# In the chunked scans of an RWKV-7 layer, VectorE masks each bank of scores before ScalarE copies from it, where ScalarE copied first

## The chip, the cores and the metric

The kernel runs on one core of a Trainium2 chip. A core has TensorE (PE, the matrix engine), VectorE (DVE), ScalarE (ACT), GpSimd (POOL) and SyncE (SP, which issues most transfers). Each engine takes its own instructions strictly in order and runs beside the others; semaphores make one wait for another. TensorE writes its results into PSUM, which has eight banks; ScalarE and VectorE read them from there. The metric is the time of one execution on the device in microseconds (us), lower being better, as the median of several runs.

## The reference

Two layers run on 2048 latent tokens with a context of 256 tokens, width 1024. Layer 0 is an RWKV-7 mixer, layer 1 a differential attention. The change lies in the scans of layer 0: for each of 16 heads of 64, in both directions of time,

```python
def step(S, inp):
    r_t, w_t, k_t, v_t, kk_t, a_t = inp
    sa = jnp.einsum("bhvk,bhk->bhv", S, kk_t)
    S = (S * w_t[:, :, None, :]
         - sa[..., None] * (kk_t * a_t)[:, :, None, :]
         + v_t[..., None] * k_t[:, :, None, :])
    return S, jnp.einsum("bhvk,bhk->bhv", S, r_t)
...
oc_f, sc_f = scan_direction(con, 0, s0, False)
oc_b, sc_b = scan_direction(con, 1, s0, True)
ol_f, _ = scan_direction(lat, 0, sc_f, False)
ol_b, _ = scan_direction(lat, 1, sc_b, True)
```

## The kernel before

A first stage projects the tokens and writes streams to HBM; `phase2` runs the scans; a readout and the attention layer follow. `phase2` works by chunks of 64 tokens: 36 chunks in each direction make 72 turns of a loop over `q`, and the two directions alternate. A turn does two things that are nine turns apart in the scan:

- **`scores` for chunk `q+9`.** Four banks of score products, g0 to g3 here, each of four matmuls (L680) into a PSUM tile `ps` named `scps`. Everything else is read out of that bank. ScalarE copies the two diagonal blocks to `A32` (L687, two copies) and an off-diagonal block to `E` (L690); these are "the copies". VectorE multiplies the bank by a causal mask, one half into `L` (L691, the tile LA for g0 and g1, LB for g2 and g3), the other half into `Pb` (L692); these are "the masks".
- **`chain` for chunk `q`.** TensorE multiplies the state by LA and LB (L796, "x", the first matmuls of a turn) into the two `xops` tiles; ScalarE copies to `X` (L798); TensorE multiplies by the inverse `U` (L804); ScalarE scales into `RS` (L807, "the RS scaling"); TensorE forms the state update (L813, needs `RS` and the keys `KB`) and the outputs (L818, needs `RS` and `Pb`); VectorE updates the state `RX` (L824, L825) and ScalarE copies the outputs (L826, "the RS copies"). There are two `xops` tiles, so the next turn's x can't begin before the first RS copy has emptied the first of them. The chunk's `v` comes by a transfer into `RS` that SP issues after it has issued the store of the turn before (L827), which waits for the RS copies.

Beside these, `turned` transposes keys into `scps` banks (L773) and ScalarE copies them to `KB` (L774), before g0 and again between g1 and g2. `scps` has three banks, taken in turn, so g2 needs the bank of g0 emptied by both its readers, and g3 that of g1.

Every four turns, the blocks of four chunks are inverted together. By `q mod 4` I call the turns kind 0 to 3:

- kind 0: `join`: VectorE negates `Dg` into `U` (L742, four instructions) between the masks of g0 and g1; TensorE joins (L749); ScalarE copies `U` (L751).
- kind 1: nothing more.
- kind 2: `unpack`: VectorE transposes the inverse (L715 before the masks of g0, L717 between those of g0 and g1, L719 between those of g2 and g3).
- kind 3: VectorE transposes `A32` to `N` for GpSimd's inversion (L699, L700) and unpacks the last piece (L721) ahead of the masks of g0; TensorE joins rows (L733); then a `join` as in kind 0. There is one `A32`, so ScalarE's first copy of this turn waits for L700.

The order of all four engines is the order in which this code is written (`in_order` fixes it), and the framework adds the waits: the second reader of a bank waits for the first, on whichever engine each is. The order of the steps in a turn is

```python
MAIN = "ubgjugbcgujgc"
```

after a first step of the chain, with u for `unpack`, b for `turned`, g for a bank of scores, j for `join`, c for the chain.

Of the kernel before, what the change touches and what calls it, by code (L numbers as in the profile page):

```python
# [15 lines left out]
ALU = mybir.AluOpType  # L16
# [17 lines left out]
def bcast(ap, dim, n):  # L34

    ap = ap.unsqueeze(dim)
    shape = list(ap.shape)
    shape[dim] = n
    return ap.broadcast_to(shape)
# [561 lines left out]
def causal_masks(k, pool):  # L601

    nc = k.nc
    mk = pool.tile([128, 2, 2, 64], F32, name="causal")
    nc.vector.memset(mk, 1.0)
    for d in range(2):
        for slot in range(2):
            strict = slot == d
            for half in range(2):
                v = mk[half * 64:half * 64 + 64, d, slot]  # L610
                step = 1 if d == 0 else -1
                nc.gpsimd.affine_select(out=v, in_=v, pattern=[[step, 64]], base=-1 if strict else 0,
                                        channel_multiplier=-step, compare_op=ALU.is_ge, fill=0.0)
    return mk
# [7 lines left out]
def phase2(k):  # L622

    nc, tc, S = k.nc, k.tc, k.S
# [3 lines left out]
    with ExitStack() as st:  # L628
# [17 lines left out]
        krow = (HI, LO)  # L646
# [22 lines left out]
        def scores(d, par, loaded, A32, E, Pb):  # L669

            LA, LB, BA, BB = loaded
            yield LA, LB, Pb
            br, kr = brow[d], krow[d]
            for ab in range(2):
                L, B = ((LA, BA), (LB, BB))[ab]
                for q in range(2):
                    ps = sc.tile([128, 4, 2, 64], F32, name="scps")
                    for j in range(4):
                        p = 4 * q + j
                        nc.tensor.matmul(f2(ps[:, j]), f2(B[:, p]), f2(L[:, p]), start=(j == 0), stop=True,  # L680
                                         skip_group_check=True)
                    prs = slice(4 * q, 4 * q + 4)
                    h0 = 8 * ab + 4 * q
                    c0 = 16 * par + h0
                    for blk in range(2):
                        r = slice(br.start + 32 * blk, br.start + 32 * blk + 32)
                        nc.scalar.copy(A32[r, :, c0:c0 + 4].rearrange("p t c -> p c t"),  # L687
                                       ps[r, :, d, 32 * blk:32 * blk + 32])
                    e, ec = (slice(0, 32), slice(32, 64)) if d == 0 else (slice(96, 128), slice(0, 32))
                    nc.scalar.copy(E[e, c0:c0 + 4, :], ps[e, :, d, ec])  # L690
                    nc.vector.tensor_tensor(L[krow[ab], prs], ps[kr], bcast(mk[kr, d], 1, 4), op=ALU.mult)  # L691
                    nc.vector.tensor_tensor(Pb[br, h0:h0 + 4], ps[br, :, 1 - d], bcast(mk[br, d, 1 - d], 1, 4),  # L692
                                            op=ALU.mult)
                    yield

        def invert(A32, eng):
# [139 lines left out]
        for i in range(LEAD + 1):  # L836
# [3 lines left out]
            if i == 0:  # L840
                mk = causal_masks(k, ca)
# [30 lines left out]
        with in_order(k, mybir.EngineType.PE, mybir.EngineType.DVE, mybir.EngineType.Activation, mybir.EngineType.Pool):  # L872
            for q in range(-LEAD, nq):
# [21 lines left out]
                if s < nq:  # L895
                    if s % 4 == 0:
                        tiles[s // 4] = [ip.tile([128, 32, 32], F32, name="A32", bufs=1),
                                         ip.tile([128, 32, 32], F32, name="E", bufs=2), None]
                    A32, E, _ = tiles[s // 4]
                    if s % 2 == 0:  # L900
                        Pb = pb.tile([128, 16, 64], F32, name="Pb")
                    g = scores(s % 2, s // 2 % 2, loaded.pop(s), A32, E, Pb)
                    prep[s] = step(g)
# [791 lines left out]
```

## Time and profile before

| | |
|---|---|
| median of 3 runs | 4957.97 us (4957.65 to 4968.01) |
| the profiled execution's own time | 4959.93 us |
| its span | 4958.2 us |
| busy over the span | PE 94%, PEld 84%, DVE 74%, ACT 54%, POOL 22% |
| mean granted TensorE clock | 0.972 |

The span is the profiled part of the execution; 1.7 us of its own time lie around it. PE is the matmuls and PEld the weight loads, which overlap them. A matmul's end is modelled, so a share of PE near 100% doesn't say that PE has nothing to gain. The scans run from 1167 us, where the first bank of scores is read, to 2273 us, where the last output is stored. A row of the time line names the engine, the line of the kernel, the operation and the tiles; what stands in brackets is how long the engine was idle before it and what ended that.

### The profile page before, as it was taken

To read this page: it belongs to the slowest core of one execution; us is meant where nothing else is said; L and a number is where in the kernel's file an instruction comes from. 1 tells how busy PE (TensorE), PEld (TensorE's weight loads), DVE (VectorE), ACT (ScalarE), POOL (GpSimd) and SP (SyncE) were. 2 spreads that over 40 slices of the span, in tenths; PEclk is the share of its full clock that TensorE was granted. 3 is DMA by queue.
4 is the path that set the end of the run, shared out by engine and by line. 5 is a ranking of instruction groups with operands and counts; after the bars stand their busy time and mean duration, and the time that the engine had idled before them with its cause. 6 is when DMAs were issued, how large, how long until landed. Compare 5 with 4: busy or idle time off the path is not lost. (4 is left out here: it accounts for less than half of the span.)

```text
span 4958.2 us, 100487 instructions
## 1 busy us (share of the span) xinstructions
PE 4642.4 (94%) x40786; PEld 4181.3 (84%) x40786; DVE 3676.0 (74%) x5933; ACT 2678.6 (54%) x4780; POOL 1110.3 (22%) x1470
## 2 busy tenths in 40 slices
PE   7999999998889998898989999999999999999989
PEld 5999999996788888876768888878888888888977
DVE  6788887888877777766768258238888888888843
ACT  4555655554666666655541221227777777777720
POOL 1121112112555665551222022010000000000000
PEclk8999999999999999999999999999999999999999
DMA  4555665557666667669853332241212112111042
GB/s 165 169 166 168 179 182 160 165 166 212 155 157 168 159 168 169 166 189 283 265 172 100 113 112 90 94 116 29 52 32 49 49 33 49 49 32 30 19 158 94
DMA packets 733584, 629.94 MB, mean 127 GB/s; under 512 B 175238, under 2 KB 638521, under 8 KB 732097
## 3 DMA queue, kind: packets, MB, share of 16 engines
q1 hardware_dynamic: 730641, 619.84, 44.1%
q8 instruction: 322, 5.28, 0.4%
q10 hardware_dynamic: 2480, 3.67, 0.3%
q14 instruction: 141, 1.16, 0.1%
HBM read 423.61 MB, written 199.77 MB: 126 GB/s over the span
## 5 line engine op out<-in xcount | busy, mean ns | idle before, releaser
L1423 ACT ACTIVATE p<-p,m 128x2304 f32<-128x2304 f32 x256 | 568.9, 2222 | 92.9 <-DVE p L1412 88.6
L1455 PE MATMUL pv<-v,at 128*128 128x128 f32 x4608 | 598.6, 275 | 3.1 <-ACT at L1450 3.0
L1455 PEld LDWEIGHTS pv<-v,at 128*128 128x128 f32 x4608 | 555.1, 192 | 4.2 <-ACT at L1450 4.2
L1409 PE MATMUL sc<-ks,qh 128*128 128x512 f32 (+1 forms) x1280 | 520.1, 406 | 5.1 <-DVE p L1412 4.2
L1450 ACT COPY at<-tps 128x512 f32<-128x512 f32 (+1 forms) x640 | 343.7, 537 | 273.8 <-PE tps L1448 272.5
L1410 PE MATMUL sc<-ks,ql 128*128 128x512 f32 (+1 forms) x1280 | 464.2, 372 | 0.0
L363 PE MATMUL mmps<-hH,wH 128*128 128x386 f32 x1632 | 433.4, 346 | 17.6 <-DVE sg L581 12.7
L363 PE MATMUL mmps<-hL,wH 128*128 128x386 f32 x1632 | 431.0, 344 | 8.4 <-DVE hL L92 8.4
L363 PE MATMUL mmps<-hH,wL 128*128 128x386 f32 x1632 | 428.1, 343 | 0.3 <-DVE nm_ss L197 0.3
L939 PE MATMUL mmps<-wH,hH 128*128 128x512 f32 x1088 | 425.1, 391 | 3.1 <-ACT hH L91 3.1
L939 PE MATMUL mmps<-wH,hL 128*128 128x512 f32 x1088 | 424.4, 390 | 1.4 <-DVE hL L92 1.4
L939 PE MATMUL mmps<-wL,hH 128*128 128x512 f32 x1088 | 424.7, 390 | 0.0
L1412 DVE TENSOR_SCALAR_CACHE_REDUCE p<-sc,m 128x1280 f32<-128x1280 f32 x256 | 396.3, 1548 | 17.5 <-PE sc L1410 1.3
L1433 DVE SCALAR_TENSOR_TENSOR p<-p,r,p 128x1152 f32<-128x1152 f32 x256 | 373.4, 1459 | 4.5
L1412 DVE TENSOR_SCALAR_CACHE_REDUCE p<-sc 128x1024 f32<-128x1024 f32 x256 | 312.6, 1221 | 62.3 <-PE sc L1410 60.4
L1448 PE MATMUL tps<-ident,p 128*128 128x128 f32 x2304 | 355.9, 272 | 0.3
L363 PEld LDWEIGHTS mmps<-hH,wH 128*128 128x128 f32 x1632 | 300.7, 193 | 21.8 <-DVE sg L581 16.1
L1486 POOL TENSOR_TENSOR o<-o,sub_y 128x512 f32<-128x512 f32 (+1 forms) x33 | 33.5, 1014 | 1272.5 <-DVE sub_y L1481 1270.6
L363 PEld LDWEIGHTS mmps<-hL,wH 128*128 128x128 f32 x1632 | 303.6, 192 | 10.4 <-DVE hL L92 9.2
L1448 PEld LDWEIGHTS tps<-ident,p 128*128 128x128 f32 x2304 | 278.0, 141 | 36.4 <-ACT at L1450 1.4
L363 PEld LDWEIGHTS mmps<-hH,wL 128*128 128x128 f32 x1632 | 304.1, 192 | 0.9 <-DVE nm_ss L197 0.8
L707 POOL TENSOR_TENSOR N<-N,rank 128x30 f32<-128x30 f32 (+14 forms) x510 | 280.0, 549 | 40.0
(309 smaller groups left out, 10348.9 us busy)
## 6 DMA issues: line engine op xcount, KB each, us to landing
wr<-in_rw_in_dram SPq DMA_DIRECT2D x102, 512.0 KB
s_qr<-QR SPq DMA_DIRECT2D x48, 768.0 KB
BK<-s_bk SPq DMA_DIRECT2D x72, 512.0 KB
s_bk<-BK SPq DMA_DIRECT2D x47, 768.0 KB
wraw<-in_da_in_dram SPq DMA_DIRECT2D x64, 512.0 KB
BA<-s_bk SPq DMA_DIRECT2D x72, 256.0 KB
LA<-s_qr SPq DMA_DIRECT2D x72, 256.0 KB
BB<-s_bk SPq DMA_DIRECT2D x72, 256.0 KB
```

The lines of the kernel that those rows point to most:

```text
L363: nc.tensor.matmul(a[:, :b1 - b0], wt[:, kt, :], ht[:, kt, b0:b1], start=(kt == 0 and wt is wH and ht is hH), stop=(kt == KT - 1 and last))
L707: eng.tensor_tensor(N[:, m + 1:32, 0:m], N[:, m + 1:32, 0:m], t, op=ALU.subtract)
L939: k.nc.tensor.matmul(ps, s(kt), m(kt), start=(kt == 0 and s is sH and m is mH), stop=(kt == KT - 1 and last))
L1409: nc.tensor.matmul(s[:, b0 - g0:b1 - g0], qh[:, cs], ks, start=True, stop=False)
L1410: nc.tensor.matmul(s[:, b0 - g0:b1 - g0], ql[:, cs], ks, start=False, stop=True)
L1412: nc.vector.tensor_scalar(tiles[n][c][:, g0:g1], s[:, :g1 - g0], -1.0, m, op0=ALU.mult, op1=ALU.min, accum_out=least)
L1423: nc.scalar.activation(P, P, AF.Exp, bias=m, scale=-1.0, accum_out=z)
L1433: nc.vector.scalar_tensor_tensor(P0[:, b0:b1], P1[:, b0:b1], r, P0[:, b0:b1], op0=ALU.mult, op1=ALU.add)
L1448: nc.tensor.transpose(ps[:, c - b0:c - b0 + 128], P0[:, c:c + 128], k.ident)
L1450: (eng.copy if eng is nc.scalar else eng.tensor_copy)(at[b][:, :b1 - b0], ps[:, :b1 - b0])
L1455: nc.tensor.matmul(acc, at[b][:, c - b0:c - b0 + 128], H.v[:, c // 128], start=(c == 0), stop=(c == T - 128))
L1486: eng.tensor_tensor(H.o[:, cs], H.o[:, cs], bcast(y[:, cs.start - t0:cs.stop - t0], 2, 128), op=ALU.mult)
```

## The change

In `scores`, the two masks on VectorE stand ahead of the three copies on ScalarE. Nothing else is altered: the instructions, their sizes and their order on each engine are the same, since the copies are ScalarE's and the masks VectorE's. What differs is who waits for whom. The line numbers move: masks L691, L692 become L685, L686, and copies L687, L690 become L690, L693.

```diff
@@ scores
                     c0 = 16 * par + h0
+                    nc.vector.tensor_tensor(L[krow[ab], prs], ps[kr], bcast(mk[kr, d], 1, 4), op=ALU.mult)
+                    nc.vector.tensor_tensor(Pb[br, h0:h0 + 4], ps[br, :, 1 - d], bcast(mk[br, d, 1 - d], 1, 4),
+                                            op=ALU.mult)
                     for blk in range(2):
                         r = slice(br.start + 32 * blk, br.start + 32 * blk + 32)
                         nc.scalar.copy(A32[r, :, c0:c0 + 4].rearrange("p t c -> p c t"),
                                        ps[r, :, d, 32 * blk:32 * blk + 32])
                     e, ec = (slice(0, 32), slice(32, 64)) if d == 0 else (slice(96, 128), slice(0, 32))
                     nc.scalar.copy(E[e, c0:c0 + 4, :], ps[e, :, d, ec])
-                    nc.vector.tensor_tensor(L[krow[ab], prs], ps[kr], bcast(mk[kr, d], 1, 4), op=ALU.mult)
-                    nc.vector.tensor_tensor(Pb[br, h0:h0 + 4], ps[br, :, 1 - d], bcast(mk[br, d, 1 - d], 1, 4),
-                                            op=ALU.mult)
                     yield
```

VectorE in a turn of kind 2 in the middle of the scans, before, with the engines that each instruction waits for (PE, Activation for ScalarE, Pool; the number behind is the program's). LA and LB take the first mask of a bank, Pb the second.

```order
L715 STREAM_TRANSPOSE Tt<-N 32x32x32 [waits Pool_49]
L691 TENSOR_TENSOR LA_11137<-scps,causal 64x512 [waits PE_49,Activation_49]
L692 TENSOR_TENSOR Pb<-scps,causal 64x256
L717 STREAM_TRANSPOSE Tt<-N 32x32x32
L691 TENSOR_TENSOR LA_11137<-scps,causal 64x512 [waits PE_49,Activation_49]
L692 TENSOR_TENSOR Pb<-scps,causal 64x256
```

The same place now.

```order
L715 STREAM_TRANSPOSE Tt<-N 32x32x32 [waits Pool_49]
L685 TENSOR_TENSOR LA_11137<-scps,causal 64x512 [waits PE_49]
L686 TENSOR_TENSOR Pb<-scps,causal 64x256
L717 STREAM_TRANSPOSE Tt<-N 32x32x32
L685 TENSOR_TENSOR LA_11137<-scps,causal 64x512 [waits PE_49]
L686 TENSOR_TENSOR Pb<-scps,causal 64x256
```

Nothing has moved; the masks' wait for ScalarE is gone, and only that for TensorE is left.

ScalarE in the same turn, before, from the copies of g1 to those of g2; the copies of g3 and the two RS copies follow in both. RS belongs to the chain, KB to the keys.

```order
L687 COPY A_18036<-scps 32x4x32 [waits PE_49]
L687 COPY A_18036<-scps 32x4x32
L690 COPY E<-scps 32x128
L774 COPY KB<-scps 128x512 [waits PE_49]
L807 ACTIVATE RS<-chps 64x512 [waits DMAHW7_49,PE_49,Activation_49]
L807 ACTIVATE RS<-chps 64x512
L687 COPY A_18036<-scps 32x4x32 [waits PE_49]
L687 COPY A_18036<-scps 32x4x32
L690 COPY E<-scps 32x128
```

The same place now.

```order
L690 COPY A_18036<-scps 32x4x32 [waits DVE_49,PE_49]
L690 COPY A_18036<-scps 32x4x32
L693 COPY E<-scps 32x128
L774 COPY KB<-scps 128x512 [waits PE_49]
L807 ACTIVATE RS<-chps 64x512 [waits DMAHW7_49,PE_49,Activation_49]
L807 ACTIVATE RS<-chps 64x512
L690 COPY A_18036<-scps 32x4x32 [waits DVE_49,PE_49]
L690 COPY A_18036<-scps 32x4x32
L693 COPY E<-scps 32x128
```

The order is the same here too; the first copy out of every bank now also waits for VectorE, and what stands behind it in ScalarE's queue (the key copy, the RS scaling, the RS copies) stands behind that wait.

## Rows read from the trace of the kernel before

**Rows 1.** Waits, 1300 to 2160 us: total us, times, longest.

```profile
DVE LA L691 <- ACT E L690: 106.3, 43, 7.0
...
PE chps L813 <- DMA RS<-s_v: 23.7, 22, 2.6
```

**Rows 2.** Groups by line, 1300 to 2160 us: busy us, mean ns of one.

```profile
L687 ACT COPY A<-scps 32x128 f32<-32x128 f32 x478 | 178.6, 374 | 60.4 <-PE scps L680 40.0 <-DVE N L700 11.8 <-PE chps L804 2.4
...
L692 DVE TENSOR_TENSOR Pb<-scps,causal 64x256 f32<-64x256 f32 x237 | 100.0, 422 | 3.2
...
L691 DVE TENSOR_TENSOR LA<-scps,causal 64x512 f32<-64x512 f32 x119 | 81.7, 686 | 107.7 <-ACT E L690 106.3
...
L774 ACT COPY KB<-scps 128x512 f32<-128x512 f32 x120 | 69.8, 582 | 1.9 <-PE scps L773 0.5
...
L826 ACT COPY RS<-xops 64x512 f32<-64x512 f32 x118 | 68.4, 579 | 129.7 <-PE xops L818 129.7
L690 ACT COPY E<-scps 32x128 f32<-32x128 f32 x238 | 65.9, 277 | 1.4
```

**Rows 3.** Time line of PE: start of x in turns 4, 32 to 36, 60.

```profile
1313.85 1.15 PE L796 MATMUL xops<-RX,LA 128*64 128x64 f32 x32
...
1720.89 1.15 PE L796 MATMUL xops<-RX,LA 128*64 128x64 f32 x32
...
1733.88 1.15 PE L796 MATMUL xops<-RX,LA 128*64 128x64 f32 x32
...
1747.16 1.15 PE L796 MATMUL xops<-RX,LA 128*64 128x64 f32 x32
...
1758.69 1.15 PE L796 MATMUL xops<-RX,LA 128*64 128x64 f32 x32
...
1775.75 1.15 PE L796 MATMUL xops<-RX,LA 128*64 128x64 f32 x32
...
2125.29 0.92 PE L796 MATMUL xops<-RX,LA 128*64 128x64 f32 x24
```

**Rows 4.** Time line of ScalarE and VectorE, turn 32 (kind 0).

```profile
1724.49 0.78 ACT L687 COPY A<-scps 32x128 f32<-32x128 f32 x2 [0.31 <-PE scps L680]
...
1726.56 2.72 DVE L742 TENSOR_SCALAR U<-Dg 32x512 f32<-32x512 f32 x4
...
1726.96 1.21 ACT L807 ACTIVATE RS<-chps 64x512 f32<-64x512 f32 x2
...
1729.81 1.16 ACT L751 COPY U<-chps 32x512 f32<-32x512 f32 x2 [0.75 <-PE chps L749]
...
1733.05 0.58 ACT L826 COPY RS<-xops 64x512 f32<-64x512 f32 x1 [1.18 <-PE xops L818]
```

**Rows 5.** Time line of PE, turn 33 (kind 1).

```profile
1744.08 1.15 PE L813 MATMUL chps<-RS,KB 128*64 128x64 f32 x32 [1.76 <-DMA RS<-s_v]
```

**Rows 6.** Time line of ScalarE and VectorE, turn 34 (kind 2).

```profile
1750.77 0.76 ACT L687 COPY A<-scps 32x128 f32<-32x128 f32 x2 [0.25 <-PE scps L680]
...
1757.13 1.96 DVE L719 STREAM_TRANSPOSE Dg<-N 64x1024 f32<-64x1024 f32 x1
```

**Rows 7.** Time line, turn 35 (kind 3).

```profile
1760.70 2.21 PE L733 MATMUL chps<-Tt,E 32*32 32x32 f32 x128
...
1766.17 1.96 DVE L721 STREAM_TRANSPOSE Dg<-N 64x1024 f32<-64x1024 f32 x1
...
1766.42 0.77 ACT L687 COPY A<-scps 32x128 f32<-32x128 f32 x2 [1.52 <-DVE N L700]
...
1769.03 1.87 DVE L742 TENSOR_SCALAR U<-Dg 32x512 f32<-32x512 f32 x4
```

**Rows 8.** Start of x in turns 27 and 28.

```profile
1641.41 1.15 PE L796 MATMUL xops<-RX,LA 128*64 128x64 f32 x32
...
1661.93 1.15 PE L796 MATMUL xops<-RX,LA 128*64 128x64 f32 x32
```

**Rows 9.** Windows, four us of turn 27: busy us by engine, PEclk, DMA share, GB/s.

```profile
1656.00:1660.00 4.00, 4.00 (x53) 3.64 (x50) 1.26 (x3) 2.13 (x5) 3.45 (x8) 0.55 0.00 0
```

## The prediction

> **What bounds the kernel now.** I began with the waits of the scans' steady part, 1300 to 2160 us [rows 1]. In 43 of 119 masks into LA VectorE sat idle until ScalarE's last copy out of the same bank, 106.3 us in all: this is the wait that the change takes away. It is no gain by itself, since nothing says that anybody waits for VectorE there. So the second view is the time line of a round of four turns, and what ends each turn: the next x, whose starts are in [rows 3]. Turns 32 to 35 lasted 12.99, 13.28, 11.53 and 17.06 us (kinds 0 to 3), 54.86 us together, a round in which the matmuls are seen at full speed. From turn 4 to turn 60, 14 rounds, it is 811.44 us, or 57.96 a round: on the average 3.10 us are lost beside it.
>
> What the reader is to see in [rows 4]: ScalarE has some room in a turn. It waited 0.75 us before the copies of `U` and 1.18 us before the first RS copy, in each case for TensorE. It is TensorE that carries the turns (in kind 1 it waits 1.76 us for the transfer of `v` [rows 5]), and ScalarE feeds it at three places of the chain. VectorE's work is in lumps: 2.72 us of `U` between the masks of g0 and g1 in kind 0 [rows 4], transposes of 1.96 us at the same place and ahead of g3's masks in kind 2 [rows 6]. Before, ScalarE ran past these lumps. Now each copy stands behind them.
>
> **The change part by part.** No instruction is added or removed; only the order within a bank turns round, so its cost is the difference of two queues. The pieces, from [rows 2]: the copies of a bank are 2 x 0.374 + 0.277 = 1.03 us, its masks 0.686 + 0.422 = 1.11, and 1.15 with the step to the next instruction; a key copy is 0.58, an RS copy 0.58. The RS scaling is 1.21 and the `U` copies 1.16 [rows 4]. I lay out each kind of turn in the times of the trace: VectorE masks as soon as the bank is there or it is free, the copies follow, everything else keeps its place.
>
> Kind 0 [rows 4]: g0 is there at 1724.49, when ScalarE took it up. Masks to 1725.64, the four L742 (2.72) to 1728.36, masks of g1 to 1729.51. ScalarE, which before had begun g1's copies by 1725.5, ends them at 1730.54, the key copy at 1731.13, the RS scaling at 1732.35 (it had ended at 1728.17), g2's copies at 1733.4, `U` at 1734.55, g3's at 1735.6, the first RS copy at 1736.2. From then on x can start, at about 1736.3 instead of 1733.88: **+2.4 us**. Is TensorE ready by then? In kind 1 the update began 3.08 us before the next x [rows 5, 3], and its second half needs the end of the scaling, so from 1732.35 it is ready 3.08 less half an update (0.54), at 1734.9. ScalarE's queue decides, by 1.4 us. The banks don't: g3 waits for g1's copies (1730.54), and ScalarE comes to g3 four us later.
>
> Kind 1: VectorE has no lump. Each bank's copies come some 1.15 us later, but the update waited 1.76 us for `v` [rows 5], and the transfer is issued behind the RS copies of the turn before, which have moved with x. The delay lies beside that wait: **0**. Without this cover it would be up to 1.15 us a turn.
>
> Kind 2 [rows 6]: g0 is there at 1750.77. Masks to 1751.92, L717 (as long as L719, 1.96) to 1753.9, g1's masks to 1755.05 and g2's to 1756.2, L719 to 1758.15, g3's to 1759.3. ScalarE: g1's copies to 1756.1, keys 1756.7, scaling 1757.9, g2's copies 1758.95, g3's, which wait for the masks, to 1760.35, RS copy 1760.95, x at 1761.05 instead of 1758.69: **+2.35**. TensorE would be ready at 1757.9 + 2.54 = 1760.45.
>
> Kind 3 [rows 7]: here something comes back. VectorE began L719 at 1757.13 and now begins at 1756.2, 0.93 earlier, and its queue from there is the same, so L721 ends at 1766.17 + 1.96 - 0.93 = 1767.2. With x at 1761.05, g0 is there 3.60 us later as in kind 0 (1724.49 - 1720.89), plus 2.21 for joining rows, at 1766.85; VectorE is last. Masks to 1768.35, the four L742 (1.87 here) to 1770.2, g1's masks to 1771.35, copies to 1772.4, keys 1773.0, scaling 1774.2, g2's copies 1775.25, `U` 1776.4, g3's 1777.45, RS copy 1778.05, x 1778.15. Before it was 1775.75, and with the 2.35 that the turn starts later 1778.10: **+0.05**. ScalarE's new wait costs what it saves by no longer waiting 1.52 us for L700.
>
> A clean round becomes 4.8 us longer. Banks are scored up to turn 62, 63 turns or 15.75 rounds, so there are 16 turns each of kinds 0 and 2 and 15 of kind 3: 16 x 2.4 + 16 x 2.35 + 15 x 0.05 = 76.8 us. In the nine turns ahead of the chain nothing on ScalarE is waited for by a chain, and I count nothing.
>
> Against this stands a part of the 3.10 us a round that are lost now, mostly in stretches at half the clock [rows 9]. TensorE gets slack of 1.4, 0.6 and 1.4 us in kinds 0, 2 and 3 (ready 1734.9, 1760.45 and 1776.75 against x), and slow matmuls ahead of such slack cost nothing. Bounds: nothing is hidden (0), or as much as the slack, all of the 3.10 (48.8 over 15.75 rounds). I take 1 us a round, a third, since a slow stretch falls anywhere in a round and the slack lies at three turns' ends: -16. **Sum: 76.8 - 16 = +61 us**, on 4959.93 of the profiled execution 5021, and as that stands 2 us above the median, **5019 us** at the median.
>
> **The rivals.** *The clock falls more often* (slower still). Each of the new waits leaves TensorE idle for one to two us. The granted clock was 0.55 over four us of turn 27 [rows 9], near the lower of its two levels of 1.2 and 2.4 GHz, and that turn lasted 20.52 us [rows 8] where one of the same kind lasted 17.06: 3.46 us for such a stretch. One more of them a round is 54.5 us: 5073. For it speaks that waits become more; against it, that waits of about this length are all over the scans now and most turns are not slowed. [...]
>
> *VectorE is the one that ends last* (faster). If the copies' delay found room, what would be left is VectorE running ahead: in kind 3 ScalarE waited 1.52 us for L700 [rows 7], and 15 times that is 22.8 us: 4935. It decides on the lump between the masks of g0 and g1: ScalarE's room in kind 0 is 0.75 + 1.18 = 1.93 us, and its g1 copies begin 4.0 us late (1729.51 against 1725.5). With a lump of 0.6 us instead of 2.72 it would be free. I see no way to that.
>
> *The waits are hidden everywhere as in kind 1* (no change, 4958): if TensorE waited for `v` in all turns. That wait is 23.7 us [rows 1] over some 60 turns (119 masks into LA, two a turn), 0.4 us a turn, against 2.4 needed.
>
> *Only one of the two kinds shows* (half: 4985 to 4995), for instance if L742 takes 1.87 us in kind 0 as it does in kind 3, and x finds the bank free sooner.
>
> **How the numbers follow.** The forecast has 0.62 (4995 to 5045 by the bounds of what is hidden and some tenths of a us in each step), the clock 0.16, half 0.07, no change 0.08, faster 0.07. A measurement here can tell some 0.2%, 10 us, from no change. So faster 0.07, same 0.09 with a little of the half, slower 0.84. The range 4985 to 5060 holds the forecast, the half and the lower part of the clock's case, about 0.8.
>
> **What would show it.** After: no wait of LA for `E`; instead ScalarE's first copy of a bank waits for `Pb`, longest before g1 in kinds 0, 2 and 3. Turns of kinds 0 and 2 last some 15.4 and 13.9 us, kinds 1 and 3 as before. PE waits for the first RS copy before x. Everything after the scans is only shifted. I'd be wrong if ScalarE still reached the RS copies before TensorE's outputs, or if kind 3 grew or shrank by more than a us.

## The result and the profile after

With the masks first the kernel takes 5030.74 us (median of 4 runs, 5024.96 to 5040.06) against 4957.81 for the kernel before (4 runs on the same chip): a ratio of 1.0142, interval 1.0121 to 1.0163, or 73 us more. The ratios here and below are estimates from all the runs and differ from the quotients of the medians by up to 0.0011. The profiled execution took 5031.1 us, with a span of 5029.4 and a mean granted clock of 0.962, where it was 0.972. Of all the executions behind the numbers below one, of the second kernel under "Which banks cost?", took 12099.97 us at a granted clock of 0.60; it is left out.

The waits of the kernel after, over the same stretch and with the same columns as [rows 1]:

```profile
ACT A L690 <- DVE Pb L686: 186.4, 108, 3.4
DVE LA L685 <- PE scps L680: 133.4, 47, 6.5
...
PEld scps L680 <- ACT E L693: 65.7, 60, 2.0
...
PE scps L680 <- ACT E L693: 50.7, 41, 1.8
ACT RS L826 <- PE xops L818: 48.8, 71, 2.1
...
PE chps L813 <- DMA RS<-s_v: 9.2, 10, 1.8
...
PE xops L796 <- ACT RS L826: 4.8, 11, 0.5
```

The wait of LA for `E` is gone, and VectorE now waits 133.4 us for the bank itself: it runs ahead of TensorE. In its place ScalarE waits 186.4 us for `Pb`. The reader should look at what stands under these: TensorE's scores (L680) now wait for `E`, up to 1.8 us at a time, a wait that the same stretch of the kernel before does not have. That is the bank of g2 or g3 being emptied too late by copies that now come last. Over turns 4 to 59 it is 20.5 us in the 14 turns of kind 0, 23.9 in those of kind 2 and 7.9 in those of kind 3, or some 1.5, 1.7 and 0.6 us a turn. ScalarE's wait for TensorE's outputs before the RS copies has gone from 129.7 us in 118 places [rows 2] to 48.8 in 71, and before x TensorE waits for the first RS copy only 4.8 us in all. The wait for `v`, the cover of kind 1, has shrunk from 23.7 to 9.2 us.

The time line of ScalarE in turn 8 (kind 0; its x starts at 1375.91), which answers to [rows 4]:

```profile
1380.72 0.76 ACT L690 COPY A<-scps 32x128 f32<-32x128 f32 x2 [1.52 <-DVE Pb L686]
...
1384.62 0.75 ACT L690 COPY A<-scps 32x128 f32<-32x128 f32 x2 [3.03 <-DVE Pb L686]
1385.19 0.29 ACT L693 COPY E<-scps 32x128 f32<-32x128 f32 x1
1385.50 0.59 ACT L774 COPY KB<-scps 128x512 f32<-128x512 f32 x1
1385.99 1.21 ACT L807 ACTIVATE RS<-chps 64x512 f32<-64x512 f32 x2
...
1390.42 0.58 ACT L826 COPY RS<-xops 64x512 f32<-64x512 f32 x1 [0.30 <-PE xops L818]
```

And VectorE beside it:

```profile
1379.51 0.68 DVE L685 TENSOR_TENSOR LA<-scps,causal 64x512 f32<-64x512 f32 x1 [2.84 <-PE scps L680]
...
1380.66 2.73 DVE L742 TENSOR_SCALAR U<-Dg 32x512 f32<-32x512 f32 x4
1383.41 0.68 DVE L685 TENSOR_TENSOR LA<-scps,causal 64x512 f32<-64x512 f32 x1
```

The lump of L742 stands between the two masks into LA, and ScalarE waits 3.03 us before g1's copies for it and for g1's masks behind it. Behind them the key copy and the RS scaling start late: 1385.99 is 10.08 us behind x, where in [rows 3, 4] it was 6.07 (1726.96 against 1720.89).

TensorE in turns 5 to 9:

```profile
1333.58 1.15 PE L796 MATMUL xops<-RX,LA 128*64 128x64 f32 x32
...
1345.42 1.15 PE L796 MATMUL xops<-RX,LA 128*64 128x64 f32 x32
...
1354.27 1.16 PE L680 MATMUL scps<-LB,BB 128*128 128x128 f32 x8 [1.79 <-ACT E L693]
...
1359.15 1.15 PE L796 MATMUL xops<-RX,LA 128*64 128x64 f32 x32
...
1375.91 1.15 PE L796 MATMUL xops<-RX,LA 128*64 128x64 f32 x32 [0.47 <-ACT RS L826]
...
1381.81 1.16 PE L680 MATMUL scps<-LB,BB 128*128 128x128 f32 x8
...
1385.53 1.91 PE L680 MATMUL scps<-LB,BB 128*128 128x128 f32 x8 [1.43 <-ACT E L693]
1387.37 1.95 PE L813 MATMUL chps<-RS,KB 128*64 128x64 f32 x32
1389.25 2.08 PE L818 MATMUL xops<-RS,Pb 64*64 64x64 f32 x32
1391.25 1.15 PE L796 MATMUL xops<-RX,LA 128*64 128x64 f32 x32
...
1400.14 1.15 PE L813 MATMUL chps<-RS,KB 128*64 128x64 f32 x32 [0.62 <-DMA RS<-s_v]
```

Two things are to be seen. Turns 5 to 7 (kinds 1 to 3) last 11.84, 13.73 and 16.76 us, so this kind 1 is shorter than the 13.28 of [rows 3]; but it is the shortest of fourteen, and their mean is 13.68. And in turn 8 TensorE waits 1.43 us for `E` before g3, and the matmuls behind that wait take 1.91 and 1.95 us, where the same forms take 1.16 and 1.15 elsewhere. From there L813, L818 and the next x follow one another without a wait. The windows (columns as in [rows 9]) of those four us and of 30 us that end ten us ahead of them:

```profile
1385.00:1389.00 4.00, 3.47 (x38) 3.25 (x40) 1.79 (x4) 3.89 (x10) 3.53 (x7) 0.59 0.17 34
...
1345.00:1375.00 30.00, 26.28 (x597) 24.44 (x595) 27.07 (x34) 19.17 (x45) 9.77 (x20) 1.00 0.65 160
```

The granted clock is 0.59 in the one, near the lower level of 1.2 GHz, and 1.00 in the other, in which TensorE had also waited 1.79 us (at 1354.27). Over turns 4 to 60, from x to x, the window of the kernel before is:

```profile
1313.85:2125.29 811.44, 726.33 (x14787) 680.42 (x14785) 629.56 (x869) 526.51 (x1232) 472.94 (x870) 0.96 0.67 165
```

and that of the kernel after:

```profile
1318.10:2193.50 875.40, 781.22 (x14786) 725.14 (x14786) 633.80 (x870) 523.51 (x1232) 466.74 (x868) 0.91 0.62 153
```

The mean round went from 57.96 to 62.53 us (875.40 / 14), and 4.57 us over 15.75 rounds are 72 us. By the traces 64 of the 71 us between the two spans lie in these turns, and 4 more ahead of turn 4. By kind, the mean of the 14 turns from x to x:

| us | kind 0 | kind 1 | kind 2 | kind 3 |
|---|---|---|---|---|
| before | 13.67 | 13.29 | 12.52 | 18.49 |
| after | 16.56 | 13.68 | 14.35 | 17.94 |

The busy time of the other engines is the same to 1.3%, but TensorE was busy 54.9 us longer with the same matmuls, at a clock of 0.91 instead of 0.96. From the two levels, a mean of 0.96 is 8% of the time at half the clock, some 65 us here, and 0.91 is 18%, some 158 us.

### The profile page after: what moved, and what is told of

It is laid out like the page before. It is cut to its first block, busy times and chain, and to the rows that moved or that the text cites. A ratio compares the mean times of both kernels' runs of the same rounds, so it can differ in the third digit from the quotient of the medians.

```text
span 5029.4 us, 100489 instructions
## 1 busy us (share of the span) xinstructions
PE 4707.4 (94%) x40786; PEld 4234.1 (84%) x40786; DVE 3681.6 (73%) x5933; ACT 2676.9 (53%) x4780; POOL 1103.2 (22%) x1470
## 3 DMA queue, kind: packets, MB, share of 16 engines
q14 instruction: 140, 1.15, 0.1%
## 5 line engine op out<-in xcount | busy, mean ns | idle before, releaser
L690 ACT COPY A<-scps 32x128 f32<-32x128 f32 x576 | 214.6, 373 | 274.8 <-DVE Pb L686 253.0
```

## The experiments

My theory was that ScalarE's queue behind VectorE's lumps makes the turns longer, and that the clock costs little. The main rival was that the new waits of TensorE bring the clock down. All ratios are to the kernel before on the same chip.

**Which banks cost?** Masks first only in g1 of kinds 0, 2 and 3, copies first in the other 13 banks of a round; then just the opposite set.

```diff
+                    first = (kind, ab, q) in ((0, 0, 1), (2, 0, 1), (3, 0, 1))
+                    if first:
+                        nc.vector.tensor_tensor(L[krow[ab], prs], ps[kr], ...)
...
+                    if not first:
+                        nc.vector.tensor_tensor(L[krow[ab], prs], ps[kr], ...)
```

In the second `first` is `not (...)` of the same.

> Masks first in one bank alone, g1, and only in the turns of kinds 0, 2 and 3, where VectorE has L742 or L717 between the masks of g0 and g1; all other banks copy first as before. If the queue behind those lumps is what costs, this is the whole cost or more, since g0's masks still wait for the copies and so the lump starts later too: 5030 to 5080 us. If each bank whose order is turned costs alike, 3 banks of 16 cost a fifth of 73 us: 4972.

> Masks first in all banks but g1 of kinds 0, 2 and 3, the opposite set. If the queue behind the lumps costs, nearly all of the 73 us come back, but for g3 of kind 2 (behind L719) and g0 of kind 3 (behind L721): 4958 to 4985 us. If each bank costs alike, 13 banks of 16: 5017.

The three banks alone: 5076.12 us, ratio 1.0229 (1.0199 to 1.0259). The other 13: 4976.09, ratio 1.0027 (1.0006 to 1.0047). So the banks behind a lump carry the cost, and alone they cost more than the whole change. The waits of the first kernel (L692 and L695 are its copies, L688 its masks ahead of the copies, L697 those behind) suggest why:

```profile
ACT A L692 <- DVE Pb L688: 187.4, 39, 5.6
DVE LB L697 <- ACT E L695: 187.2, 78, 3.9
PEld scps L680 <- ACT E L695: 83.9, 39, 3.1
```

ScalarE waits as long for VectorE as in the whole change, and then VectorE waits for ScalarE in g2 and g3, where in the whole change it does not: behind a lump, two queues that are crossed in one turn hold each other up twice. The clock has a part in this too. Over turns 4 to 60 (columns as in [rows 9]) it was 0.87, and TensorE was busy 79 us longer than before with the same matmuls, of the 100 us by which these turns grew:

```profile
1321.16:2232.69 911.53, 805.62 (x14786) 750.57 (x14785) 631.91 (x869) 522.12 (x1232) 468.14 (x869) 0.87 0.57 148
```

**Is it the lump, by its place?** The first join step, with L742, is moved behind g1 in both orders (after, then before).

```diff
-MAIN = "ubgjugbcgujgc"
+MAIN = "ubgugjbcgujgc"
```

> The changed kernel with the first join step moved behind g1's scores and masks, so that the four L742 no longer stand between the masks of g0 and g1; kind 2 as in the changed kernel. If the lumps cost, kinds 0 and 3 fall by about 2 us each while kind 2 stays, and the join waits for U a little: 4975 to 5000 us. If each bank costs alike: 5031 plus what the join then waits, 5031 to 5050.

> The kernel before with the same move of the join step: what the move itself costs. The join matmuls wait for U about a us longer in kinds 0 and 3, by either theory: 4965 to 4990 us. With the lump out of the way, masks first against copies first would then be about kind 2's part alone, 10 to 30 us; if each bank costs alike, still 73.

Masks first: 4967.78, ratio 1.0015 (0.9998 to 1.0032). Copies first: 4985.87, ratio 1.0052 (1.0032 to 1.0072). With L742 behind g1, masks first is 18 us faster than copies first; I had expected it slower by 10 to 30, and the pair missed that. What I had left out stands in the waits of the second kernel:

```profile
PEld chps L749 <- DVE U L742: 52.4, 60, 1.6
PE chps L749 <- DVE U L742: 43.3, 60, 1.4
```

The join now waits for `U`, because VectorE comes to L742 only after g1's copies. With masks first VectorE runs ahead, and the first of these waits is 18.2 us in the other kernel. Of the 73 us, 63 are gone by moving a lump of 2.7 us past one bank.

**Is it the lump, by its size?** L742 is left out after the first round, in both orders.

```diff
+        seen = set()
...
-            for g in range(4):
+            for g in range(4 if par not in seen else 0):
...
+            seen.add(par)
```

> The changed kernel with the four L742 left out in all rounds but the first, so that U keeps old values on its diagonal (part of the computation is left out). If the queue behind the lumps is what costs, kinds 0 and 3 lose their lump and only kind 2 pays: some 15 to 35 us above its copies-first twin. The time itself also falls by what L742 costs on any path.

> The copies-first twin of the last: the kernel before with the same four L742 left out. Its join no longer waits for U: 4910 to 4945 us. The difference of the two is 15 to 35 us if the lumps cost, and still about 73 if each bank costs alike.

Masks first: 4978.93, ratio 1.0028 (1.0012 to 1.0044). Copies first: 4952.09, ratio 0.9981 (0.9963 to 0.9998). They are 26.8 us apart, inside the 15 to 35 expected for kind 2 alone; the copies-first kernel gained only 0.19%, where I had looked for a time of 4910 to 4945 us, so L742 was nearly free before. By difference the lump of L742 makes some 46 of the 73 us, with what the clock does behind it.

**What is the clock's part?** L804 is issued a second time, with the same operands into the same place, so that TensorE has other work in each turn; in the kernel after, and as a control in the kernel before.

```diff
-            for p in range(8):
+            for p in (*range(8), *range(8)):
```

> The changed kernel with the L804 matmuls of each turn issued twice (the same values written again), 1.1 us more of TensorE's work in each turn, just ahead of the place where it stands idle in kinds 0, 2 and 3. If a good part of the loss is the clock that falls in that idle time, half-clock stretches become fewer and the time stays within 10 us of the changed kernel or falls below it, though 72 turns get 1.1 us more work. If the loss is the queue alone, the extra work is hidden in kinds 0, 2 and 3 and shows in kind 1: 5031 to 5050, with the clock as it was. If TensorE's own work carries the turns, 72 x 1.1 = 79 us more: 5110.

> The control for the doubled matmuls: the kernel before, copies first, with L804 issued twice. If the clock is the whole loss and the queue behind the lumps costs nothing once the clock holds, this comes out as the doubled masks-first kernel did, about 4957 us. If the queue costs some 2.9 us in a round at full clock (57.7 against 54.9 us in undisturbed rounds), it is some 30 to 45 us faster, if the extra matmuls are hidden here too: 4912 to 4927. If TensorE carries the turns here, as the transfers and the joins leave it little room, the extra work shows: up to 79 us on an undisturbed 4909, 4960 to 4988.

After, with more work: 4956.71, ratio 0.9994 (0.9981 to 1.0007), 74 us **faster** than without it. Before, with more work: 4944.46, ratio 0.9969 (0.9952 to 0.9985), which is none of the three outcomes that I had laid out for it. The first of the two over turns 4 to 60:

```profile
1309.80:2122.10 812.30, 760.13 (x16576) 708.65 (x16576) 631.31 (x868) 520.21 (x1233) 468.50 (x870) 1.00 0.63 166
```

and the control:

```profile
1303.90:2103.10 799.20, 761.88 (x16579) 720.10 (x16577) 631.83 (x871) 527.24 (x1232) 479.33 (x876) 0.97 0.68 167
```

The clock is 1.00 in the one and 0.97 in the other, and masks first is then 12.25 us behind copies first (4956.71 against 4944.46, on two chips) instead of 73. The control's profiled execution, 4928.09 us, was the fastest of its ten. The second L804 does more than hold the clock: it also takes away most of the wait for `v`, in the control from 23.7 us to

```profile
PE chps L813 <- DMA RS<-s_v: 3.5, 5, 1.7
```

and in the kernel after, where it was 9.2, all of it. In the kernel after with L804 twice the waits for `Pb` are as large as ever:

```profile
ACT A L690 <- DVE Pb L686: 209.6, 130, 3.3
...
PE scps L680 <- ACT E L693: 22.9, 37, 0.9
```

but TensorE's own wait behind them is at most 0.9 us instead of 1.8: the second L804 lies in it. The round of turns 32 to 35 of that kernel, at full clock throughout:

```profile
1715.79 1.15 PE L796 MATMUL xops<-RX,LA 128*64 128x64 f32 x32 [0.47 <-ACT RS L826]
...
1720.62 2.08 PE L804 MATMUL chps<-X,U 128*64 128x64 f32 x64
...
1730.70 1.15 PE L796 MATMUL xops<-RX,LA 128*64 128x64 f32 x32 [0.39 <-ACT RS L826]
...
1742.65 1.15 PE L796 MATMUL xops<-RX,LA 128*64 128x64 f32 x32
...
1756.72 1.15 PE L796 MATMUL xops<-RX,LA 128*64 128x64 f32 x32
...
1773.50 1.15 PE L796 MATMUL xops<-RX,LA 128*64 128x64 f32 x32 [0.47 <-ACT RS L826]
```

Kinds 0 to 3 last 14.91, 11.95, 14.07 and 16.78 us there, 57.71 together. Kinds 1 to 3 agree with turns 5 to 7 of the kernel after, which has no second L804, to 0.34 us. One round is a small sample, so here are the means of all those turns from 4 to 59 in which the granted clock was 1.00 from x to x, with their number out of 14:

| us | kind 0 | kind 1 | kind 2 | kind 3 |
|---|---|---|---|---|
| before | 13.29 (11) | 13.10 (12) | 12.12 (11) | 17.31 (5) |
| after | none | 12.58 (5) | 13.82 (10) | 16.91 (10) |
| before, L804 twice | 13.47 (11) | 12.11 (13) | 12.46 (14) | 17.62 (6) |
| after, L804 twice | 14.94 (14) | 11.96 (14) | 13.89 (14) | 17.11 (13) |

The order of the readers makes kinds 0 and 2 longer and kind 3 a little shorter. Kind 1 of some 12 us is not its doing: the control, copies first, has it too.

**A version from this.** Masks first only where no lump stands in the way: g0 of kind 0, and all of kind 2 with its two transposes L717 and L719 moved behind the masks of g1 and g3; then the same with L804 twice.

```diff
+                    first = kind == 2 or (kind, ab, q) == (0, 0, 0)
...
-                for at, name in enumerate(MAIN):
+                for at, name in enumerate("ubggujbcgjguc" if q % 4 in (2,) else "ubgjugbcgujgc"):
```

> Masks first only where no lump stands ahead of them: g0 of kind 0, and all four banks of kind 2, in which L717 and L719 are moved behind the masks of g1 and of g3. All other banks copy first. If the lumps are what costs, this has the good half of the change without the bad: U is ready 0.9 us sooner in kind 0, VectorE's queue is earlier at the end of kind 2 so that ScalarE waits less for L700 in kind 3: 4925 to 4950 us. If each bank costs alike, 5 of 16: 4981.

> The kernel with masks first where no lump stands ahead of them, and L804 issued twice. It has 34 us at half clock in 14 rounds now, so the clock can give back at most some 20 us, and the extra work costs up to 79 where TensorE carries a turn (kind 1 waits for a transfer, kinds 2 and 3 partly for ScalarE): 4925 to 4970 us; below 4940 only if the extra work is hidden in most turns.

4940.29 us, ratio 0.9957 (0.9943 to 0.9971), and with L804 twice 4933.04, ratio 0.9954 (0.9940 to 0.9968): both beat the kernel before by intervals that leave 1 out, and the second L804 adds nothing that these intervals tell. The window of the first over turns 4 to 60:

```profile
1309.90:2101.90 792.00, 714.49 (x14788) 666.70 (x14786) 628.23 (x869) 522.89 (x1232) 478.99 (x869) 0.98 0.69 169
```

The mean round is 56.57 us and the clock 0.98, higher than before. Of its waits, 1300 to 2160 us, two are taken up below: that for `v`, and that of the first copies for L700, here L706 (the lines behind the masks move by 6):

```profile
PE chps L819 <- DMA RS<-s_v: 25.3, 21, 2.4
...
ACT A L692 <- DVE N L706: 2.2, 6, 0.4
```

## Why the prediction held, and where its steps did not

It forecast 5019 us, slower, by ScalarE's queue; it is 5030.74. The sum was +61 and the difference is 73, but that they are so near is luck: the queue's term was too large and the clock's had the wrong sign, and each was wrong by more than the 12 us between the sums.

- **The wait that moves, right.** LA's wait for `E` is gone, ScalarE waits for `Pb` before g1 (3.03 us in turn 8), and what stands behind it in the queue comes late. There g1's copies end 9.57 us behind x (1385.19 + 0.29 - 1375.91), where 9.65 was forecast. The experiments on the place and the size of L742 show that this lump is the larger part.
- **What ends a turn, right only at full clock.** "ScalarE's queue decides" and "the banks don't" put TensorE's spare time at a turn's end, before x. In the kernel after it lies earlier, before the scores, for a bank (50.7 us against 4.8 before x), and behind it TensorE can still end last. In turn 8 ScalarE waited 0.30 us for TensorE before the first RS copy, the prediction's own sign of being wrong, and the list has 71 such waits. With L804 twice, at a clock of 1.00, the list has none, and x does wait for the RS copy behind kinds 3 and 0 (0.47 us at the start of turn 32, 0.39 at that of turn 33), though not behind kind 2.
- **Kind 0, too large.** +2.4 forecast, 14.94 - 13.29 = +1.65, the first with L804 twice, since after the change no turn of kind 0 was at full clock. One step that failed is the price of a bank's copies, 1.03 us as the sum of three durations: neighbours in ScalarE's queue overlap, and g1's three copies of turn 8 took 1385.50 - 1384.62 = 0.88 us. The RS scaling likewise began 0.10 us before the key copy ended.
- **Kind 2, somewhat too large.** +2.35 forecast, 13.82 - 12.12 = +1.70. The turn itself was forecast well, at 13.9 us; the 11.53 that it was held against is short for its kind. Kind 3, forecast +0.05, came to -0.40.
- **Kind 1, small as forecast.** 0 forecast; by the means of all turns +0.39, by those at full clock 12.58 - 13.10 = -0.52. But its cover is not fixed, as the prediction took it to be: the wait for `v` fell from 23.7 to 9.2 us. Why is open. The transfers' share of the engines fell too, from 0.67 to 0.62, but the wait does not follow this share: it is 3.5 us at 0.68 in the control, and 25.3 at 0.69 in the version of the last experiment.
- **The clean round** grew by 1.65 - 0.52 + 1.70 - 0.40 = 2.43 us, not 4.8: 38 us over 15.75 rounds instead of 76.8. Some 1 us of the excess is the one round that the forecast stood on: turns 32 to 35 took 54.86 us, and the four means of the kernel before add up to 55.82.
- **The half clock, wrong in sign.** "Slow matmuls ahead of such slack cost nothing" was to give back 16 us. What a mean round loses beside the four means rose from 57.96 - 55.82 = 2.14 us to 62.53 - 58.25 = 4.28 (58.25 with kind 0 as above), so by these means it cost 2.14 x 15.75 = 34 us, the rest of the 72 of the trace. The failed step counted only that TensorE would have time to spare at a turn's end. The rows show slow matmuls behind the spare time, as in turn 8, and with that time partly filled the clock went from 0.91 to 1.00.

So the rival "the clock falls more often" was half right: right in mechanism, and sized at one more stretch of 3.46 us a round where these means give 2.14. The Trainium skill (TensorE: Matmul & The Clock Gate, "A second HAM failure mode: psum-queue depth-cycling") tells of a kernel that goes round its PSUM banks, in which TensorE's short idle times between groups of matmuls come often enough that the clock goes to and fro between its levels. Here too the waits are for a bank, and the clock of 0.91 against 0.96, and of 1.00 with the waits shortened, agrees.

How much of the 73 us is the clock's stays an estimate. By the means at full clock it is 34 us, but turns picked by their clock are not picked at random, and kind 0 had to be taken from another kernel. The two kernels with L804 twice, read in the same way, differ by 1.47 - 0.15 + 1.43 - 0.51 = 2.24 us a round, or 35 us for the queue. Their times differ by 12 us only, which would leave up to 61 for the clock; but there the control's clock was 0.97, not 1.00, and the second L804 also touches the wait for `v`. No run separated these.

The rival on the other side, VectorE ending last, needed a lump below 0.6 us ahead of g1. With L742 behind g1 masks first is the faster of the two by 18 us, but there the join also waits less for `U`, and it does not beat the kernel before (1.0015, 0.9998 to 1.0032). The version of the last experiment does, by 0.43%, and in it ScalarE's wait for the transposes of `A32` has gone from the 11.8 us of [rows 2] to 2.2, as this rival has it. That version mixes two edits, the order in a bank and the place of L717 and L719, which no run took apart.

## What to carry to other kernels

When two in-order engines read the same bank, the order of the readers ties their queues together: put first the engine whose queue has no long instruction just ahead, bank by bank if need be. Crossing the order within a turn was worst behind a lump (1.0229); the last version, faster than the kernel before, crosses it in kind 0, where no lump stands ahead. A cover of one turn (here the wait for `v`) is not a constant: it went from 23.7 us to 9.2 with the order of two readers, and to 3.5 with 32 matmuls more a turn. One round of a trace is a thin base for a forecast; take the mean of many, and sort the turns by their clock first. Where TensorE has short waits in every turn, look at the granted clock before counting slack as harmless, and try a harmless repeat of matmuls to see what the clock is worth.

## What was unexpected of the hardware

A kernel became 74 us faster (5030.74 to 4956.71) by issuing 32 matmuls twice in each turn, 2.08 us for 64, which is some 1.04 us more work in each of 72 turns. In the control the same edit gave 0.31%.

Half-clock stretches came in a kernel whose longest listed wait of TensorE for `E` in the scans is 2.0 us (on the weight loads; 1.8 on the matmuls), and not behind every one: the 30 us ahead of turn 8 are at 1.00 and hold such waits too. Nor does the length of the wait tell: in the kernel after, none of the 14 turns of kind 0 was at 1.00 throughout, and ten of the 14 of kind 2 were, though the wait for `E` is longer in kind 2 (1.7 against 1.5 us a turn). Which of them bring the clock down is not settled by these runs.
